# Masks from a row-xor-column table, a second bank ring for one early projection, and new TensorE costs in a list schedule

## The chip, the cores and the metric

The kernel runs on one core of a Trainium2 chip. The metric is the device time of one execution in microseconds (us); of several runs the median is given. Engines are named as in the profile: PE (TensorE), PEld (its weight loads), DVE (VectorE), ACT (ScalarE), POOL (GpSimd), SP (SyncE, which issues most DMAs).

## The reference, cut to what matters

One decoder block, 1024 tokens of width 1024, all in float32:

```python
proj = rms_norm(x, norm1_g) @ w_in            # q, k, v, hq, hf, hi, hg, two gates
o_sb = stick_breaking_attention(q, k, v)      # 8 heads of 64, strictly causal
o_hg = hgrn2_mixer(q_hg, f_hg, i_hg, g_hg)    # 4 heads of 128, a gated recurrence in chunks
mixed = sigmoid(gate_sb) * (o_sb @ w_b[:512]) + sigmoid(gate_hg) * (o_hg @ w_b[512:])
h = x + mixed @ w_out
out = h + (silu(hn @ w_gate) * (hn @ w_up)) @ w_down      # hn = rms_norm(h, norm2_g)
```

In the recurrence, `attn[t, s]` within a chunk is `sum_k q[t,k] key[s,k] exp(b[t,k] - b[s,k])` for `s <= t`, where `b` is a running sum of `log f`.

## The kernel before, in words

**Products.** A float32 product is made from three products in a rounded format (`fp32r`): each operand is split into a high part (`ah`, `oh`, `th`, ...; ACT or POOL rounds it) and a low part (`al`, `ol`, `tl`, ...; DVE subtracts). One such triple over 512 columns is the unit of the large projections. Some smaller products and all transposes run in full fp32: the transposes (through `ident`), the level products of the recurrence (`ms<-dl`), its state updates (`ms<-xi,tail`) and outputs (`ms<-tail,state`, `ms<-kb,xi`).

**Stages.** (1) x is loaded in two halves of 512 tokens, scaled by the norm's gain and split into `ah` and `al`; its squares are added up in `tail` on DVE, and a product with ones gives the sums. (2) 44 weight tiles of `w_in` give q, k, v, hq, hf, hi, hg of four pairs of heads or heads, and 16 gate tiles. Each is one call of `proj` for each half: eight steps of three matmuls into one PSUM bank. Between them run `scores`, `values` and `hgrn` for each of four steps. (3) The branch products, the output product and the FFN's first half, the latter by a Winograd scheme of seven products instead of eight. (4) The down projection, written out by hand in program order.

**The list schedule.** Stages 1 to 3 aren't issued in program order. `Plan.op` records every instruction with its engine, a planned duration, a rank and its dependencies; `Plan.issue` then simulates the engines with these durations and issues each engine's instructions in the order in which the simulation starts them. On each engine the ready instruction of highest rank goes first, then the one with the longest way to the end of its stage. The projections have rank -1 on PE, so they are filled in where nothing else is ready; an op may also have an earliest planned time (`plan.at`). The planned durations only set the order: on the chip each engine runs its queue in that order and waits by semaphores. PE's ops are made by `M` (a group of matmuls, by columns, or with a given `us`) and `T` (a group of transposes); V, A and G make those of DVE, ACT and POOL. A new duration for PE therefore changes no instruction, but may change every queue's order.

**Rings.** Buffers come from rings of fixed size, and the simulation holds an op back until there is a free one. PSUM has three: `pj` (3 banks: projections), `z` (2: scores) and `ms` (3: everything small). `tmp` has two SBUF buffers.

**The start.** The first two weight tiles (q and k of the first pair) are projected together for the first half of x, then each for the second half; all four results take a `pj` bank in turn. `take` then reads a bank with DVE into `aa` or `vx`.

**The masks.** In each of the eight recurrence steps (four heads, two halves) seven levels m = 64, ..., 1 copy a level's product into the score tile `at` (a buffer of `kb`) where a mask says that row and column lie in the same block of m (`copy_predicated` with `mk`). The seven masks of 128 x 256 bytes are made once by `level_masks` on POOL: a memset and four `affine_select` each.

**Groups by the code.** The scores have 96 steps (four pairs, two heads each, twelve tiles), each two matmuls, 16 of them 128 columns wide. The values have 22 transpose groups for each pair and 32 products over a diagonal tile in all, four matmuls each over 768 columns together. The recurrence has 16 transpose groups (`tmp`, `tail`) and 64 full-fp32 groups: 48 levels, eight state updates, eight outputs.

Of the kernel before, what the change touches and what calls it, by code (L numbers as in the profile page):

```python
# [10 lines left out]
F32 = mybir.dt.float32  # L11
F32R = mybir.dt.float32r
I8 = mybir.dt.int8
U8 = mybir.dt.uint8
AF = mybir.ActivationFunctionType
ALU = mybir.AluOpType
# [3 lines left out]
P = 128  # L20
# [203 lines left out]
def hybrid_block(ctx: ExitStack, tc, xT, wi, wb, wo, wg, wu, wd, vec, outT):  # L224
    nc = tc.nc
# [45 lines left out]
    const1 = c1.enter_context(tc.tile_pool(name="const1", bufs=1, side="right"))  # L271
    ident = const1.tile([P, P], F32, name="ident")
    ones_r = const.tile([P, P], F32R, name="ones_r")
    bones_r = const1.tile([P, P], F32R, name="bones_r")
    future = [const1.tile([P, P], I8, name=f"future{i}") for i in range(2)]
    never = const1.tile([P, P], F32, name="never")
# [43 lines left out]
    def hs(h):  # L320
        return slice(h * HALF, (h + 1) * HALF)
# [55 lines left out]

    future = [f.bitcast(U8) for f in future]


    plan = Plan()
# [29 lines left out]
    def open_pools(phase):  # L411
        def pool(name, stack, right=False):
            pools[name] = stack.enter_context(tc.tile_pool(
                name=name, bufs=1, reuse_waits="tile", **(dict(side="right") if right else {})))

        while now[0] < phase:
            now[0] += 1
            if now[0] == 2:
                c1.close()
                st1.close()  # L420
                pool("op", st2, True)
                pool("mt", st2, True)
            elif now[0] == 3:
                tst.close()
                xst.close()
                pool("wot", ctx)
                pool("mx", mst)
            elif now[0] == 4:
                st2.close()
                rst.close()  # L430
                pool("s2p", fst, True)
                pool("fp", fst, True)
            elif now[0] == 5:
                mst.close()
                pool("preB", ctx)
                pool("wA", sta)
                pool("fa", sta)

    def new(ring, shape=(P, HALF), dt=F32):
        pool, cap, tag, phase = where[ring]  # L440
        plan.ring(ring, cap)

        def make():
            open_pools(phase)
            return (pools[pool] if phase else pool).tile(list(shape), dt, tag=tag, bufs=cap, name=tag)

        return Buf(ring, make, phase)

    def fixed(tile):
        return Buf(None, lambda: tile)  # L450
# [5 lines left out]
    def V(fn, *args, n=HALF, aps=0, rank=0, part=False, holds=(), after=(), **kw):  # L456
        cycles = 2 * n if fn == nc.vector.tensor_tensor_scan else n
        us = 0.067 + cycles / 960 + 0.061 * aps
        return plan.op("V", us, [(fn, args, kw)], rank, after, part=part, holds=holds)

    def G(fn, *args, us, rank=0, after=(), holds=(), **kw):
        return plan.op("G", us, [(fn, args, kw)], rank, after, holds=holds)

    def M(cols, mms, rank=0, after=(), holds=(), us=None):

        return plan.op("P", us or cols / 2255 + 0.003 * len(mms),
                       [(nc.tensor.matmul, m[:3], dict(start=m[3], stop=m[4])) for m in mms],
                       rank, after, holds=holds)

    def T(outs, after=(), holds=()):  # L470

        return plan.op("P", 0.11 * len(outs) - 0.08, [(nc.tensor.transpose, (o, i, ident), {})
                                               for o, i in outs], 0, after, holds=holds)


# [13 lines left out]
    act, tt = nc.scalar.activation, nc.vector.tensor_tensor  # L489
    stt, ts = nc.vector.scalar_tensor_tensor, nc.vector.tensor_scalar  # L490
# [17 lines left out]

    def level_masks():

        for m in LEVELS:
            mk = const1.tile([P, 2 * P], I8, name=f"mk{m}")
            mask = fixed(mk)
            G(nc.gpsimd.memset, mask, 1.0, us=0.15, after=(last_split[0],))
            for a in range(2):
                part = mask[:, a * P:(a + 1) * P].rearrange("p (n m) -> p n m", m=m)
                G(nc.gpsimd.affine_select, out=part, in_=part, pattern=[[-m, P // m], [0, m]],
                  compare_op=ALU.is_ge, fill=0.0, base=0, channel_multiplier=1, us=0.5)
                G(nc.gpsimd.affine_select, out=part, in_=part, pattern=[[m, P // m], [0, m]],
                  compare_op=ALU.is_ge, fill=0.0, base=m - 1, channel_multiplier=-1, us=0.5)  # L520
            lvl_mask.append(mask.bitcast(U8))


# [3 lines left out]
    last_load, last_split = [None], [None]  # L527
# [14 lines left out]
    def take_w(col, early=False):  # L542
        w = new("w", (P, 1024))
        load(w, wi[col], 512)
        return [split_w(w[:, 512 * i:512 * i + 512], early) for i in range(2)]

    def take_x(h):
        ss, acc, ws, sqs = new("ms"), new("tail"), [[], []], []
        if h == 0:
            plan.ring("kb", 4)  # L550
            for u in range(2):
                w = Buf("kb", lambda u=u: first_w[u])
                hi, lo = new("oh", dt=F32R), new("ol", dt=F32R)
                plan.at[A(nc.scalar.copy, hi, w, rank=3)] = 2.4 + 0.6 * u
                V(tt, lo, w, hi.bitcast(F32), op=ALU.subtract, rank=2)
                ws[u].append((hi, lo))
        for k in range(KT):
            x = new("aa" if h == 0 else ("xf", "xq", "xi", "xg")[k // 2])
            load(x, xT[k][:, hs(h)], 256)
            if h == 0 and k in (2, 3):  # L560
                u = k - 2
                n, v = fill[u]
                w = new("kb")
                load(w, wi[COL[n] + v][:, HALF:], 256)
                ws[u].append(split_w(w, True))
            g = vt[:, V_N1 + k:V_N1 + k + 1]
            A(act, xh[k][h][:, hs(h)], x, AF.Copy, scale=g, aps=1, rank=2 - h)
            V(stt, xl[k][h][:, hs(h)], x, g, xh[k][h][:, hs(h)].bitcast(F32), op0=ALU.mult,
              op1=ALU.subtract, aps=1, rank=2 - h)
            if k == 0:  # L570
                A(act, acc, x, AF.Square, rank=1 - h)
            else:
                sq = new("ww")
                A(act, sq, x, AF.Square, rank=1 - h)
                sqs.append(sq)
        for sq in sqs:
            V(tt, acc, acc, sq, op=ALU.add, rank=1 - h)
        M(2048, [(ss, ones, acc, True, True)])
        rstd(rr[h], ss, D, rank=1 - h)
        return ws  # L580

    last_fill = [None]

    def proj(ws, h, after=None):

        pss = [new("pj") for _ in ws]
        for k in range(KT):
            cols = slice(k % 4 * P, (k % 4 + 1) * P)
            for ps, w in zip(pss, ws):
                hi, lo = w[k // 4]  # L590
                last_fill[0] = M(1536, [
                    (ps, hi[:, cols], xh[k][h][:, hs(h)], k == 0, False),
                    (ps, hi[:, cols], xl[k][h][:, hs(h)], False, False),
                    (ps, lo[:, cols], xh[k][h][:, hs(h)], False, k == KT - 1)],
                    rank=-1, after=(last_fill[0], after))
            after = None
        return pss
# [257 lines left out]
    fill = list(fill_cols)  # L855
# [11 lines left out]
    for i, (nm, u) in enumerate(fill):  # L867
        if i == 0:
            ws = take_x(0)
            take_x(1)  # L870
            level_masks()
            pss = [proj(ws, 0)] + [proj([w], 1) for w in ws]
            for (n, v), h, ps in zip(fill[:2] * 2, (0, 0, 1, 1), sum(pss, [])):
                take(n, v, h, ps)
        elif i > 1:
            plan.part = "G" if nm == "G" else "s1"
            w = take_w(COL[nm] + u, i < 4)
            for h in range(2):
                gate = None
                if nm != "G" and u:  # L880
                    d = heads[u - 1]
                    gate = d["free " + nm] if nm in "qkv" else d["free " + nm, h]
                take(nm, u, h, proj([w], h, gate)[0])
            if nm == "hg":
                plan.part = "s1"
                ends = [f(u, e) for f, e in zip((scores, values, hgrn), ends)]
# [38 lines left out]
    for i in range(KT):  # L925
        w = get_w(wb[i])
# [27 lines left out]
    for i in range(4):  # L954
# [6 lines left out]
        for e in range(2):  # L961
            k = i + 4 * e
            w = get_w(wo[seq.pop(0)])
# [308 lines left out]
```

## Time and profile before

| | us |
|---|---|
| median of three runs (lowest, highest) | 1497.53 (1497.42, 1497.81) |
| the profiled execution | 1499.36 |
| its span, first to last instruction | 1497.6 |
| PE busy in it | 1481.0 |
| DVE, ACT, POOL busy | 1197.1, 808.4, 113.2 |

Rows are read so: in the timeline, start, duration, engine, line of the code, operation, tiles written and read (buffer numbers left out), shape, count, and in brackets how long the engine was idle before it and what ended that. In groups, after the count: busy us, mean ns of one, then idle time before them. In waits: who waited for whom, us in total, times, longest. Almost every instruction of the list schedule has line 203, where `Plan.issue` calls it, so tiles tell them apart. The modelled duration of a matmul (0.39 us for 512 columns) is longer than the step from one to the next; steps are read from the starts.

### The profile page before, as it was taken

How to read it: one execution, taken by the hardware profiler on the slowest of the kernel's cores; microseconds unless marked ns; L12 is line 12 of the kernel's file. 1: busy time of each engine (PE TensorE's matmuls, PEld its weight loads, DVE VectorE, ACT ScalarE, POOL GpSimd, SP SyncE). 2: the span in 40 equal slices, each digit the busy share in tenths (PEclk: the TensorE clock that was granted, in tenths of full speed). 3: DMA queues.
4: the chain of work that ended last, by engine and by line, in shares of the span. 5: the costliest groups of instructions: out<-in, count | busy, mean ns of one | idle time of the engine just before them, and what ended most of it. 6: DMA issues, size and time to landing. Idle time of an engine off the chain costs nothing.

```text
span 1497.6 us, 20158 instructions
## 1 busy us (share of the span) xinstructions
PE 1481.0 (99%) x7021; PEld 1224.7 (82%) x7021; DVE 1197.1 (80%) x2102; ACT 808.4 (54%) x1515; POOL 113.2 (8%) x164
## 2 busy tenths in 40 slices
PE   8999999999999999999999999999999999999999
PEld 6778888888888888888888888888888888788887
DVE  9899788988899776978867798888888888575553
ACT  7976878758868877545334453333333333354442
POOL 6111101111112001100000000000000000000000
PEclk9999999999999999999999999999999999999999
DMA  5111111111111121226434345444444455797672
GB/s 183 42 52 52 62 34 47 49 40 60 51 56 47 55 68 50 70 102 242 154 112 158 103 161 174 163 162 163 163 164 167 166 169 181 263 315 228 195 222 87
DMA packets 83157, 188.50 MB, mean 126 GB/s; under 512 B 9584, under 2 KB 11632, under 8 KB 83056
## 3 DMA queue, kind: packets, MB, share of 16 engines
q1 hardware_dynamic: 72400, 167.82, 33.6%
q10 hardware_dynamic: 10656, 19.40, 3.5%
q8 instruction: 55, 0.90, 0.3%
q14 instruction: 46, 0.38, 0.1%
HBM read 131.61 MB, written 55.57 MB: 125 GB/s over the span
## 4 chain that ended last, share of the span: by engine, by line
PE 76%; DVE 8%; ACT 2%; issue 2%; DMA 0%; POOL 0%; DVEq 0%; POOLq 0%; ACTq 0%
PE pj L203 33%; PE ms L203 17%; PE f L1180 14%; PE z L203 12%; DVE dl L203 2%; DVE kb L203 1%; DVE aa L203 1%; DVE ol L203 1%; ACT aa L203 1%; DVE tl L203 1%; DVE ww L203 1%; DMA rb<-act_d 0%; ACT ww L203 0%; ACT qhh L203 0%; ACT tmp L203 0%
## 5 line engine op out<-in xcount | busy, mean ns | idle before, releaser
L203 PE MATMUL pj<-ah,oh 128*128 128x512 f32 x704 | 286.9, 407 | 1.4 <-DVE aa L203 1.0
L203 PE MATMUL pj<-al,oh 128*128 128x512 f32 x704 | 276.0, 392 | 2.2 <-DVE al L203 2.2
L203 PE MATMUL pj<-ah,ol 128*128 128x512 f32 x704 | 276.3, 392 | 0.0
L203 ACT CAST oh<-w 128x512 fp32r<-128x512 f32 x168 | 102.2, 621 | 243.4 <-PE ms L203 84.0
L203 DVE TENSOR_TENSOR ol<-w,oh 128x512 fp32r<-128x512 f32 x248 | 170.1, 690 | 15.5 <-POOL oh L203 10.3
L203 PE MATMUL ms<-f,oh 128*128 128x512 f32 x528 | 162.7, 389 | 0.2 <-DVE g L203 0.2
L203 PEld LDWEIGHTS pj<-ah,ol 128*128 128x128 f32 x704 | 132.5, 188 | 29.2
L203 PEld LDWEIGHTS pj<-al,oh 128*128 128x128 f32 x704 | 133.1, 189 | 25.7 <-DVE al L203 4.0
L203 PEld LDWEIGHTS pj<-ah,oh 128*128 128x128 f32 x704 | 133.0, 189 | 23.8 <-DVE aa L203 1.4
L1180 PE MATMUL f<-bh,ah 128*128 128x512 f32 x296 | 115.3, 389 | 1.3 <-ACT bh L256 1.3
L203 PEld LDWEIGHTS ms<-f,oh 128*128 128x128 f32 x528 | 99.0, 188 | 21.1 <-DVE g L203 0.6
L1180 PE MATMUL f<-bl,ah 128*128 128x512 f32 x296 | 115.4, 390 | 0.2 <-DVE bl L257 0.2
L1180 PE MATMUL f<-bh,al 128*128 128x512 f32 x296 | 115.1, 389 | 0.0
L203 DVE TENSOR_TENSOR_SCAN aa<-aa,ww 128x512 f32<-128x512 f32 (+3 forms) x96 | 93.0, 985 | 19.8 <-ACT aa L203 14.6
L203 PE MATMUL pj<-f,oh 128*128 128x512 f32 x352 | 108.4, 389 | 0.0
L203 PE MATMUL z<-f,oh 128*128 128x512 f32 x352 | 108.4, 389 | 0.0
L257 DVE TENSOR_TENSOR al<-ra,ah 128x512 fp32r<-128x512 f32 x73 | 50.5, 691 | 71.3 <-ACT ah L256 71.2
L203 PE MATMUL ms<-f,ol 128*128 128x512 f32 x264 | 102.7, 389 | 0.0
L256 ACT CAST ah<-ra 128x512 fp32r<-128x512 f32 x73 | 45.5, 624 | 96.8 <-PE f L1180 86.7
L203 POOL TENSOR_SCALAR oh<-w 128x512 fp32r<-128x512 f32 x80 | 62.3, 779 | 426.2 <-PE pj L203 332.7
L203 PE MATMUL pj<-mx,oh 128*128 128x512 f32 x256 | 78.8, 389 | 0.0
L203 PEld LDWEIGHTS pj<-f,oh 128*128 128x128 f32 x352 | 66.1, 188 | 13.7
(256 smaller groups left out, 3141.4 us busy)
## 6 DMA issues: line engine op xcount, KB each, us to landing
w<-wi SPq DMA_DIRECT2D x42, 512.0 KB, 3.7
rb<-act_d SPq DMA_DIRECT2D x73, 256.0 KB, 4.2
w<-wg SPq DMA_DIRECT2D x22, 512.0 KB, 3.6
w<-wu SPq DMA_DIRECT2D x22, 512.0 KB, 3.9
w<-wd SPq DMA_DIRECT2D x22, 512.0 KB, 4.6
wd_d<-ds SPq DMA_DIRECT2D x44, 256.0 KB, 2.9
ra<-wd_d SPq DMA_DIRECT2D x44, 256.0 KB, 4.2
act_d<-c SPq DMA_DIRECT2D x40, 256.0 KB, 4.7
```

What stands on the lines that cost most here:

```text
L203: fn(*[a.real() if isinstance(a, View) else a for a in args], **{k: v.real() if isinstance(v, View) else v for k, v in kw.items()})
L256: pin(nc.scalar.copy(hi, src))
L257: pin(nc.vector.tensor_tensor(lo, src, hi.bitcast(F32), op=ALU.subtract))
L1180: nc.tensor.matmul(banks[SET[o]][d], l[:, ws], r, start=start and i == 0, stop=p == NP - 1 and i == 2, skip_group_check=True)
```

## The change

```diff
+    TURN = 0.087
+
     def M(cols, mms, rank=0, after=(), holds=(), us=None):
-        return plan.op("P", us or cols / 2255 + 0.003 * len(mms),
+        short = max(0.0, 0.112 * len(mms) - cols / 2255)
+        return plan.op("P", us + TURN if us else cols / 2255 + max(short, 0.003 * len(mms)),
                        [(nc.tensor.matmul, m[:3], dict(start=m[3], stop=m[4])) for m in mms],
                        rank, after, holds=holds)

     def T(outs, after=(), holds=()):
-        return plan.op("P", 0.11 * len(outs) - 0.08, [(nc.tensor.transpose, (o, i, ident), {})
+        return plan.op("P", 0.109 * len(outs) + TURN, [(nc.tensor.transpose, (o, i, ident), {})
                                                for o, i in outs], 0, after, holds=holds)

     def level_masks():
+        apart = const1.tile([P, 2 * P], I32, name="apart")
+        column, row = (new("tmp").bitcast(I32)[:, :2 * P] for _ in range(2))
+        G(nc.gpsimd.iota, column, us=0.4, pattern=[[0, 2], [1, P]], base=0, channel_multiplier=0)
+        G(nc.gpsimd.iota, row, us=0.4, pattern=[[0, 2 * P]], base=0, channel_multiplier=1)
+        apart = fixed(apart)
+        V(tt, apart, row, column, op=ALU.bitwise_xor, n=2 * P)
         for m in LEVELS:
-            mk = const1.tile([P, 2 * P], I8, name=f"mk{m}")
-            mask = fixed(mk)
-            G(nc.gpsimd.memset, mask, 1.0, us=0.15, after=(last_split[0],))
-            for a in range(2):
-                part = mask[:, a * P:(a + 1) * P].rearrange("p (n m) -> p n m", m=m)
-                G(nc.gpsimd.affine_select, out=part, in_=part, pattern=[[-m, P // m], [0, m]],
-                  compare_op=ALU.is_ge, fill=0.0, base=0, channel_multiplier=1, us=0.5)
-                G(nc.gpsimd.affine_select, out=part, in_=part, pattern=[[m, P // m], [0, m]],
-                  compare_op=ALU.is_ge, fill=0.0, base=m - 1, channel_multiplier=-1, us=0.5)
+            mask = fixed(const1.tile([P, 2 * P], I8, name=f"mk{m}"))
+            plan.at[V(ts, mask, apart, float(m), None, op0=ALU.is_lt, n=2 * P)] = 45.0
             lvl_mask.append(mask.bitcast(U8))

-    def proj(ws, h, after=None):
-        pss = [new("pj") for _ in ws]
+    def proj(ws, h, after=None, ring="pj"):
+        pss = [new(ring) for _ in ws]
...
-            pss = [proj(ws, 0)] + [proj([w], 1) for w in ws]
+            pss = [proj(ws, 0)] + [proj([w], 1, ring=r) for w, r in zip(ws, ("pj", "z"))]
```

Two numbers lie in the same aligned block of m, a power of two, exactly when their xor is below m. So one table of row xor column (two iotas on POOL, one xor on DVE) gives all seven masks by one DVE compare each. They are held back to 45 us of planned time. POOL's 35 mask instructions go.

Of the first four projections, k's for the second half now takes a `z` bank.

In the list, n transposes are planned as 0.109 n + 0.087 us in place of 0.11 n - 0.08, and the full-fp32 groups with a given `us` get 0.087 more. A group of n matmuls given by columns is planned as at least 0.112 n. For triples of 512 columns this is the same 0.69 us as before.

More of the change, by code (lines that the diff above doesn't have):

```diff
@@ L13 @@
 I8 = mybir.dt.int8
+I32 = mybir.dt.int32
 U8 = mybir.dt.uint8
```

## The prediction

> **What bounds the kernel now.** I read the page's busy shares first, then the busy time of each engine in three stretches, then PE's waits in the first two stretches.
>
> ```profile
> PE 1481.0 (99%) x7021; PEld 1224.7 (82%) x7021; DVE 1197.1 (80%) x2102; ACT 808.4 (54%) x1515; POOL 113.2 (8%) x164
> 0.00:60.00 60.00, 54.28 (x217) 41.26 (x218) 52.01 (x95) 48.89 (x91) 26.56 (x50) 0.97 0.37 132
> 60.00:700.00 640.00, 634.37 (x3317) 529.18 (x3316) 546.73 (x1046) 468.56 (x941) 86.64 (x114) 1.00 0.20 65
> 700.00:1497.60 797.60, 792.30 (x3490) 654.30 (x3488) 598.37 (x962) 290.91 (x484) 0.00 (x0) 1.00 0.52 174
> ...
> PE pj L203 <- DVE al L203: 2.2, 2, 1.5
> ...
> PE pj L203 <- DVE aa L203: 1.0, 1, 1.0
> ...
> PE ms L203 <- DVE kb L203: 1.6, 6, 0.4
> PE ms L203 <- DVE tl L203: 1.5, 4, 0.7
> ```
>
> The columns of the stretches are PE, PEld, DVE, ACT and POOL busy, then granted clock, DMA share and GB/s. PE is the bound: it idles 5.7 us before 60 us, 5.6 us from 60 to 700 and 5.3 us after that, 16.6 of 1497.6 us. Nothing here takes work from PE, so all it can win or lose is PE's waiting. The edits act in the first two stretches: the start, where PE waits for `al` (the low half of x) and once for `aa` (a bank being read), and the body of the scheduled stage, where it waits briefly, mostly for DVE. After 700 us the planned costs are unchanged (three 512-column matmuls still plan as 0.69), so I put that part at zero; its cover is none but PE's own queue, and if it moves, it moves by a part of its 5.3 us.
>
> **The masks, at the start.**
>
> ```profile
> L203 POOL TENSOR_SCALAR_AFFINE_SELECT mk<-mk 128x128 int8<-128x128 int8 x28 | 19.9, 744 | 0.0
> L203 POOL MEMSET mk<- 128x256 int8 x7 | 2.1, 305 | 0.0
> ...
> 3.27 0.94 POOL L368 MEMSET qlz<- 64x1024 f32 x1
> ...
> 4.16 0.16 DVE L311 TENSOR_TENSOR e<-e,e 128x4 f32<-128x4 f32 x1 [0.30 <-ACT e L310]
> ...
> 4.57 0.91 DVE L313 TENSOR_TENSOR lb<-e,e 128x4 f32<-128x4 f32 x1
> 5.51 1.03 DVE L314 TENSOR_SCALAR omlb<-lb 128x4 f32<-128x4 f32 x1
> ...
> L203 DVE SCALAR_TENSOR_TENSOR al<-aa,vt,ah 128x512 fp32r<-128x512 f32 x8 | 6.8, 873 | 0.0
> L203 DVE SCALAR_TENSOR_TENSOR al<-xg,vt,ah 128x512 fp32r<-128x512 f32 x2 | 1.4, 741 | 0.0
> L203 DVE TENSOR_TENSOR ol<-kb,oh 128x512 fp32r<-128x512 f32 x4 | 3.5, 878 | 0.0
> L203 DVE TENSOR_TENSOR tail<-tail,ww 128x512 f32<-128x512 f32 x7 | 5.6, 797 | 0.3
> L203 DVE TENSOR_TENSOR tail<-tail,ww 128x512 f32<-128x512 f32 x7 | 4.8, 683 | 0.1
> ...
> 10.00:20.00 10.00, 10.00 (x42) 8.21 (x41) 9.69 (x14) 10.00 (x19) 10.00 (x15) 0.91 0.94 360
> ```
>
> 28 selects and 7 memsets, 22 us of POOL, leave. They hid under everything else except DVE, whose instructions are longer while they run: `lb` takes 0.91 and `omlb` 1.03 where the like step before takes 0.16; `al` 873 ns against 741 once POOL is idle; `tail` 797 (4.5 to 27.5 us) against 683 (later); `ol` 878 against the same 683. That is 1.6 + 8 x 0.13 + 7 x 0.11 + 4 x 0.20 = 4.2 us of DVE in rows shown, and some 1.0 more if the `al` of the second half lose as much: 5.2 us, an estimate. DVE cannot keep all of it, as ACT, which makes the inputs, is busy 10.00 of 10 us from 10 to 20; I keep two thirds, 3.4.
>
> What comes instead: two iotas on POOL, which is free of `qlz` at 4.2 us. The trace has no iota. The nearest rows for their ends are a 256-column memset, 0.31, and the 1024-column one, 0.94; I take 0.5 each, nearer the equal width. The xor then ends the wait of DVE at 4.2 + 1.0 + 0.4 = 5.6 us (4.8 to 6.5), and in the list it stands ahead of the first `ol` and `al`, so both queue behind it. The two `tmp` buffers that the iotas fill are free again at the xor, before the first gate asks for one; SP and ACT get nothing new. Then seven compares on DVE, held back in the list to 45 us, with DVE's work for q, k and v queued behind them:
>
> ```profile
> L203 DVE TENSOR_TENSOR dl<-dl,kb 128x256 f32<-128x256 f32 x56 | 23.0, 431 | 0.1
> L203 DVE TENSOR_SCALAR f<-f,vt 128x512 f32<-128x512 f32 x12 | 5.8, 483 | 0.1
> ...
> 6.86 0.89 DVE L203 SCALAR_TENSOR_TENSOR al<-aa,vt,ah 128x512 fp32r<-128x512 f32 x1
> ...
> 7.81 0.50 PE L203 MATMUL pj<-al,oh 128*128 128x512 f32 x1 [1.49 <-DVE al L203]
> ...
> 21.95 0.50 PE L203 MATMUL pj<-al,oh 128*128 128x512 f32 x1 [0.69 <-DVE al L203]
> ...
> 28.13 0.40 PE L203 MATMUL pj<-ah,ol 128*128 128x512 f32 x1
> 29.51 0.50 PE L203 MATMUL pj<-ah,oh 128*128 128x512 f32 x1 [0.98 <-DVE aa L203]
> 29.85 0.39 PE L203 MATMUL pj<-al,oh 128*128 128x512 f32 x1
> 30.08 0.40 PE L203 MATMUL pj<-ah,ol 128*128 128x512 f32 x1
> ```
>
> A compare has one tensor input; the one-input row is 0.48 for twice the columns, so it lies between half of that, 0.24, and the two-input 0.43 at its width. I take 0.3, nearer its kind: 2.1 us. The Trainium skill ("VectorE: DVE Perf Modes", Mode 2×_2P) lets a one-input instruction between SBUF tensors run two results per cycle, and "SBUF — State Buffer", Who interferes with whom, says that in this mode it blocks against GpSimd. By the first the seven would cost an estimated 1.4 us and the sum would be 0.5 lower; by the second, a POOL conversion of weights nearby could hold them up; no run here shows the compare yet.
>
> On PE: the first `al` comes at 7.75 now; behind the xor at 5.6 follow 0.7 of `ol` and 0.7 of `al`, about 7.0, so the wait of 1.49 loses 0.7. The wait at 21.95 (0.69, and 0.16 that hides in the modelled end of a matmul, busy 0.39 at a pitch of 0.23, as 29.85 to 30.08) goes: 0.85.
>
> **The fourth projection in another ring.** k's second half needs a fourth `pj` bank and gets it when DVE has read the first: 28.13 to 29.51 is 1.38 where 0.23 is normal, and the next step is 0.11 late: 1.26 us. With a bank of `z`, which the scores take only later in the list, it starts at once. Late next is then the weight for v, whose split DVE finishes earlier too.
>
> Start: 0.7 + 0.85 + 1.26 = 2.8 us earlier on PE. Against it: DVE is 3.4 earlier but then pays 2.1 for compares and is only some 1.3 ahead when the scores begin. Fill (projections whose weights are there) has to bridge the rest; I let 0.4 of it fail. If that cover were gone, the 1.5 us between PE's gain and DVE's would be lost. **Start: -2.4 us**, bounds -5 (its 5.7 idle but the unavoidable first wait) and 0 (xor at 6.5, compares all in PE's way).
>
> **The list's costs.** These issue nothing; they move the order. By the code there are 104 groups of transposes (22 a head in the values, 16 in the recurrence's inputs and keys), 64 other full-fp32 groups, 32 diagonal value products and 16 narrow scores. The question is whether the new costs are the trace's:
>
> ```profile
> 558.50 0.60 PE L203 MATMUL ms<-ident,tmp 128*128 128x128 f32 x4
> 558.86 0.36 PE L203 MATMUL ms<-th,vv 128*128 128x256 f32 x1
> 559.06 0.28 PE L203 MATMUL ms<-tl,vv 128*128 128x256 f32 x1
> 559.18 0.29 PE L203 MATMUL ms<-th,vv 128*128 128x256 f32 x1
> ...
> 650.48 0.61 PE L203 MATMUL ms<-dl 128*128 128x128 f32 x4
> 650.84 0.48 PE L203 MATMUL pj<-ah,oh 128*128 128x512 f32 x1
> 651.15 0.39 PE L203 MATMUL pj<-al,oh 128*128 128x512 f32 x1
> ```
>
> Four transposes: the next matmul starts 0.36 later (the old cost), and the one after it 0.20 later, not 0.12. Both together are 0.56, less 0.12 for the value matmul: **0.44**. The old list says 0.36, the new one 0.523. The level's fp32 group: 650.48 to 651.15 is 0.67, less 0.23: 0.44, the old cost; the new one says 0.527. So TURN books the late second step without the early first one. Transposes went from 0.08 too short to 0.08 too long, fp32 groups from right to 0.087 too long; only the short products (32 x 0.095 + 16 x 0.104 = 4.7 us) became right.
>
> What follows: where the list thinks PE slow, it lays less fill between a product and its consumer, and PE arrives before DVE. Fill comes in pieces of 3 x 0.23 = 0.69, so a consumer's spare time lies anywhere from 0 to 0.69. Taking 0.163 from it costs on average 0.163² / 1.38 = 0.02 us, 104 times 2.0; 0.087 from 64 others 0.4: 2.4 us. If two transposes and an fp32 group lie under one wait (0.41), it is 0.12 each time, over half of the 96 score steps of the code 6: with the rest 8, the upper end. The lower end takes away the 5.6 us idle of the body. DVE, whose order was drawn up for a PE too fast, now waits less for it: I credit 1.0. **List: +1.4 us.**
>
> Sum: 1497.6 - 2.4 + 1.4 = 1496.6. The execution with the profile lasted 1499.4 with 1.8 outside the span; the median of the runs is 1497.5, so 1.0 less there is **1496.5 us**.
>
> **Rivals.** *The list heals the body's waits*: the 5.6 us idle there are mostly DVE results late against a plan; if the new order removes all, 1497.5 - 2.4 - 5.6 = 1489.5. For it: 4.7 us of short products that are now right. Against: the rows above. Chance 0.26.
>
> *The clock stays up at the start.*
>
> ```profile
> 8.00:9.00 1.00, 1.00 (x4) 0.82 (x4) 1.00 (x2) 1.00 (x3) 1.00 (x3) 0.74 1.05 395
> 9.00:10.00 1.00, 1.00 (x4) 0.72 (x4) 1.00 (x3) 0.97 (x3) 1.00 (x2) 0.50 1.06 406
> ...
> 11.00:12.00 1.00, 1.00 (x4) 0.80 (x3) 1.00 (x3) 1.00 (x3) 1.00 (x3) 0.56 1.05 406
> ```
>
> From about 8.5 to 11.9 us the granted clock is 0.50, after PE's wait before 7.81. A shorter wait could leave it at full: half of 3.4 us, 1.7 less, 1494.8. If not, earlier matmuls merely run in the slow time, as my 0.7 assumes. The Trainium skill ("TensorE: Matmul & The Clock Gate", What's actually happening) has a gate that judges activity over free-running windows of 3.4 us; the length agrees with the dip here. Chance 0.10, half of it faster.
>
> *Slower: the thinner cover decides.* The double-booked turn starves PE at the score steps, +8: 1497.5 - 2.4 + 8 = 1503.1. It makes the kernel slower by 0.2% from 5.4 us on, a stall of 0.06 at each of the 96 steps. For it: DVE is busy 546.73 of 640 us and cannot hurry much. Against: a PE that waits once gives slack to what follows. Chance 0.22.
>
> **Chances.** 0.2%, 3.0 us, is what a measurement of this kernel can tell. My forecast holds 0.42, its own range 1493.5 to 1500, of which 0.04 falls under 1494.5. Faster: 0.26 + 0.05 + 0.04 = 0.35; same 0.43; slower 0.22. The range of 1489.5 to 1503 spans the cases.
>
> **What would show it.** POOL idle after its iotas until the first weights that it converts; `al` near 741 ns; no PE wait for `aa` near 29 us; the `al` wait under 1 us; seven compares near 0.3 us at some 45 us or later. For the list: more PE idle from 60 to 700 us than 5.6, at `z` and `ms` for DVE. I am wrong if that idle falls below 4 or rises over 9, or if the start keeps its 5.7 us.

## The result, and the profile after

The changed kernel takes **1513.3 us** (median of four, 1512.87 to 1513.75) beside 1497.47 before: a ratio of 1.0103 [1.0091, 1.0115], slower by 15.8 us. The profiled execution lasted 1512.87, its span 1511.2.

The page's busy shares and the three stretches of the changed kernel (columns as before: PE, PEld, DVE, ACT, POOL, clock):

```profile
PE 1487.3 (98%) x7021; PEld 1220.9 (81%) x7021; DVE 1196.5 (79%) x2110; ACT 807.3 (53%) x1515; POOL 99.1 (7%) x131
0.00:60.00 60.00, 56.37 (x234) 43.40 (x235) 51.99 (x107) 52.82 (x100) 6.50 (x19) 1.00 0.37 132
60.00:700.00 640.00, 624.52 (x3236) 511.02 (x3235) 533.35 (x1024) 455.88 (x922) 92.62 (x113) 1.00 0.18 59
700.00:1511.20 811.20, 806.45 (x3555) 666.48 (x3553) 611.14 (x981) 298.61 (x495) 0.00 (x0) 1.00 0.52 176
```

PE's idle time goes from 5.7, 5.6 and 5.3 us to **3.6, 15.5 and 4.7**. The start won, the body lost, the rest stayed. The span grew by 13.6: idle 10 - 2.1 - 0.6 = 7.3, and 6.3 more "busy" for the same 7021 matmuls. The clock in the first stretch is 1.00 instead of 0.97, worth 60 x 0.03 = 1.8, so the matmuls of the body show 8.1 more. That too is waiting: a 512-column matmul counts 0.39 where the next starts after 0.23, and when nothing follows, the other 0.16 counts as busy. So the body costs about 9.9 + 8.1 = 18 us and the start gives back some 4. The places in the trace agree: the last projection matmul (`pj<-ah,oh`) starts at 701.49 us where it started at 686.88, 14.6 later in spite of the start, and from there to the end it is 809.7 us where it was 810.8.

PE's waits from 60 to 700 us, after:

```profile
PE z L204 <- DVE ww L204: 7.9, 16, 1.7
PE ms L204 <- DVE kb L204: 3.3, 7, 0.8
PE ms L204 <- DVE tl L204: 1.7, 5, 0.5
PE ms L204 <- ACT tail L204: 1.0, 2, 0.6
```

`z` for `ww` is a score product waiting for a bank that DVE has yet to read (`ww<-z,aa`): 7.9 us in 16 waits, where the same view of the kernel before has

```profile
PE z L203 <- DVE ww L203: 0.5, 2, 0.3
```

The longest of them now, in the timeline:

```profile
366.01 0.72 POOL L204 TENSOR_SCALAR oh<-w 128x512 fp32r<-128x512 f32 x1 [2.12 <-PE pj L204]
366.23 1.03 DVE L204 TENSOR_TENSOR ol<-w,oh 128x512 fp32r<-128x512 f32 x1
367.19 0.41 DVE L204 TENSOR_TENSOR_SCAN kb<-tmp 128x128 f32<-128x128 f32 x1
...
368.88 0.68 DVE L204 TENSOR_TENSOR ol<-w,oh 128x512 fp32r<-128x512 f32 x1
369.47 0.41 DVE L204 TENSOR_TENSOR_SCAN kb<-tmp 128x128 f32<-128x128 f32 x1
369.81 0.66 DVE L204 TENSOR_TENSOR ww<-z,aa 128x512 f32<-128x512 f32 x1
...
370.52 0.38 PE L204 MATMUL z<-khl,qhh 128*128 128x256 f32 x1 [1.66 <-DVE ww L204]
```

DVE runs without a pause up to the `ww` for which PE stands. The same `ol` takes 0.96 from its start to the next while POOL converts an `oh` beside it, and 0.59 at 368.88; the list plans 0.60. (The Trainium skill, "SBUF — State Buffer", Who interferes with whom, has a DVE instruction with two SBUF inputs contend with a GpSimd instruction that reads SBUF; these rows agree.) Over all DVE instructions between 60 and 700 us that follow one another without a gap, the time from start to start, summed over the trace, is 430.0 us where the code's planned durations give 409.7: **5.0% slower than planned**. In the kernel before it is 432.4 against 414.3, 4.4%. Nearly all of that lies beside POOL. Of these instructions in the changed kernel, the 166 that overlap a POOL instruction by more than 0.05 us took 109.1 us where 91.2 are planned, 20% more; the other 673 took 320.9 where 318.5 are planned. In the kernel before it is 89.7 against 74.5, and 342.8 against 339.8.

The start, after:

```profile
4.15 0.63 POOL L204 IOTA tmp<- 128x256 int32 x2
4.29 0.22 DVE L315 TENSOR_SCALAR omlb<-lb 128x4 f32<-128x4 f32 x1
...
4.81 0.43 DVE L204 TENSOR_TENSOR apart<-tmp 128x256 int32<-128x256 int32 x1
5.15 0.68 DVE L204 TENSOR_TENSOR ol<-kb,oh 128x512 fp32r<-128x512 f32 x1
...
5.75 0.74 DVE L204 SCALAR_TENSOR_TENSOR al<-aa,vt,ah 128x512 fp32r<-128x512 f32 x1
...
6.55 0.50 PE L204 MATMUL pj<-al,oh 128*128 128x512 f32 x1 [0.33 <-DVE al L204]
...
20.38 0.50 PE L204 MATMUL pj<-al,oh 128*128 128x512 f32 x1 [0.30 <-DVE al L204]
...
25.16 0.39 PE L204 MATMUL pj<-ah,ol 128*128 128x512 f32 x1
25.38 0.39 PE L204 MATMUL z<-ah,oh 128*128 128x512 f32 x1
...
41.78 0.72 POOL L204 TENSOR_SCALAR oh<-w 128x512 fp32r<-128x512 f32 x1 [37.00 <-PE pj L204]
```

The xor starts at 4.81, `al` takes 0.74, PE waits 0.33 in place of 1.49, and the fourth projection enters its `z` bank at 25.38 with no wait. The compares:

```profile
49.80 0.69 DVE L204 TENSOR_SCALAR mk<-apart 128x256 int8<-128x256 int32 x3
50.76 1.08 DVE L204 TENSOR_TENSOR_SCAN aa<-aa,ww 128x256 f32<-128x256 f32 x2 [0.27 <-ACT aa L204]
51.75 0.60 DVE L204 TENSOR_TENSOR ww<-z,aa 128x256 f32<-128x256 f32 x2
...
52.20 0.44 PE L204 MATMUL z<-khl,qhh 128*128 128x384 f32 x1 [1.12 <-DVE ww L204]
52.26 0.68 DVE L204 TENSOR_TENSOR vv<-ms,vv 128x512 fp32r<-128x512 f32 x1
52.86 0.28 DVE L204 TENSOR_SCALAR mk<-apart 128x256 int8<-128x256 int32 x1
53.06 0.57 DVE L204 COPY_PREDICATED z<-future,never 128x128 f32<-128x128 uint8 x2
```

One takes 0.20 from its start to the next (52.86 to 53.06). The 0.27 of DVE's pause at 50.76 shows that the three at 49.80 delayed nothing.

### The profile page after: what moved, and what is told of

Its sections match the earlier page's. It is cut to its first block, busy times and chain, and to the rows that moved or that the text cites. A ratio compares the mean times of both kernels' runs of the same rounds, so it can differ in the third digit from the quotient of the medians.

```text
span 1511.2 us, 20128 instructions
## 1 busy us (share of the span) xinstructions
PE 1487.3 (98%) x7021; PEld 1220.9 (81%) x7021; DVE 1196.5 (79%) x2110; ACT 807.3 (53%) x1515; POOL 99.1 (7%) x131
## 4 chain that ended last, share of the span: by engine, by line
PE 71%; DVE 12%; ACT 6%; issue 2%; POOL 0%; ACTq 0%; DVEq 0%; POOLq 0%
PE pj L204 29%; PE ms L204 16%; PE f L1184 14%; PE z L204 12%; ACT aa L204 3%; DVE aa L204 2%; DVE dl L204 2%; DVE ol L204 1%; DVE tl L204 1%; DVE kb L204 1%; DVE ww L204 1%; ACT ww L204 1%; ACT qhh L204 1%; DVE tail L204 0%; DVE tmp L204 0%
## 5 line engine op out<-in xcount | busy, mean ns | idle before, releaser
L204 PE MATMUL pj<-ah,oh 128*128 128x512 f32 x696 | 283.1, 407 | 0.1
L204 PE MATMUL pj<-al,oh 128*128 128x512 f32 x696 | 272.1, 391 | 0.9 <-DVE al L204 0.9
L204 PE MATMUL pj<-ah,ol 128*128 128x512 f32 x696 | 272.6, 392 | 0.0
L204 PEld LDWEIGHTS pj<-ah,oh 128*128 128x128 f32 x696 | 131.1, 188 | 22.4 <-ACT ah L204 1.4
L204 POOL TENSOR_SCALAR oh<-w 128x512 fp32r<-128x512 f32 x80 | 68.1, 851 | 445.4 <-PE pj L204 349.1
L204 PEld LDWEIGHTS z<-f,oh 128*128 128x128 f32 x352 | 66.1, 188 | 13.7
```

The costliest lines, as they stand in the source:

```text
L204: fn(*[a.real() if isinstance(a, View) else a for a in args], **{k: v.real() if isinstance(v, View) else v for k, v in kw.items()})
```

## The experiments

Each kernel ran beside the kernel before on the same chip, whose medians were 1498.54, 1498.71, 1498.07, 1497.62 and 1498.44 us in the five groups below. Measured are the median, its ratio to the kernel before with a 95% interval, and PE's idle time from 60 to 700 us (640 less the PE figure of that stretch), 5.6 before and 15.5 after the change.

### First group: which part of the change

Theory A is the prediction's own finding made larger: the turn of a transpose is booked twice, PE's plan is too slow, and DVE comes late. B: any new order is a throw of dice. C: the short products do it. D: the new masks or the `z` bank do it.

**Masks and ring alone**, planned costs as before:

```diff
-        return plan.op("P", us + TURN if us else cols / 2255 + max(short, 0.003 * len(mms)),
+        return plan.op("P", us if us else cols / 2255 + 0.003 * len(mms),
...
-        return plan.op("P", 0.109 * len(outs) + TURN, [(nc.tensor.transpose, (o, i, ident), {})
+        return plan.op("P", 0.11 * len(outs) - 0.08, [(nc.tensor.transpose, (o, i, ident), {})
```

> The masks and the extra ring with the list's old costs. Theory A (the new costs book the turn twice, so PE is planned too slow and arrives early at the score steps): the start keeps its gain of some 4 us over the kernel before and the body stays near 5.6 us of PE idle, so 1492 to 1496 us. Theory B (any new order is a throw of the dice, and the order before was a lucky one): the masks move every queue too, so 1500 to 1512 us. Theory D (the compares or the z bank disturb the scores): near 1510 us, with the waits of z for ww.

1499.86, 1.0012 [1.0002, 1.0021], idle 8.0. This misses A's 1492 to 1496 and lies just under B's range. The start is as good as in the changed kernel, but what follows gives it back:

```profile
0.00:60.00 60.00, 56.75 (x232) 44.23 (x233) 51.52 (x106) 51.03 (x96) 6.64 (x18) 1.00 0.38 132
60.00:700.00 640.00, 632.01 (x3299) 524.85 (x3298) 537.52 (x1036) 464.33 (x934) 87.78 (x113) 1.00 0.19 64
```

**The list's costs alone**, masks by POOL and the fourth projection in `pj` (`level_masks` and `proj` as before; `M` and `T` as changed):

> The new list costs alone, masks and ring as before. Theory A: all of the loss and none of the start's gain, 1513 + 4 = 1515 to 1519 us, waits of z for ww as after. Theory B: anywhere from 1495 to 1515. Theory D: near 1498 us.

1518.62, 1.0132 [1.0117, 1.0147], idle 12.5. The loss is the list's; D falls. PE's waits are spread otherwise here (`ms` for `tl` 4.5 us, `z` for `ww` 3.7). A part of the loss may be this list's own: it leaves PE 4.5 us without work between 107 and 115 us of planned time, where the changed kernel's list has no gap, and in its trace the granted clock is 0.91 from 120 to 140 us.

**True transposes**: their cost as read from the trace (0.44 for four), full-fp32 groups as before, short products as changed.

```diff
-        return plan.op("P", us + TURN if us else cols / 2255 + max(short, 0.003 * len(mms)),
+        return plan.op("P", us if us else cols / 2255 + max(short, 0.003 * len(mms)),
...
-        return plan.op("P", 0.109 * len(outs) + TURN, [(nc.tensor.transpose, (o, i, ident), {})
+        return plan.op("P", 0.109 * len(outs) + 0.008, [(nc.tensor.transpose, (o, i, ident), {})
```

> As the changed kernel, but a transpose group is planned as 0.109 n + 0.008 and a full-fp32 group as before, which is what the starts in the trace of before add up to; the short products keep their new costs. Theory A: the double booking is gone, so 1494 to 1500 us. Theory B: 1500 to 1512. Theory C (it is the short products, now right, that take the cover from the scores): 1508 to 1515.

1500.83, 1.0014 [1.0004, 1.0023], idle 8.5: just above A's range and inside B's, far below C's.

**Old transposes**, the other two costs as changed (`T` alone as before, 0.11 n - 0.08):

> As the changed kernel, but the transposes keep the old cost, 0.11 n - 0.08; fp32 groups with the turn and short products as changed. Theory A: the larger part of the overbooking (104 x 0.163 of 27 us planned) is gone, so 1496 to 1504 us. Theory C: 1508 to 1515.

1500.88, 1.0013 [1.0003, 1.0022], idle 8.5. The full-fp32 groups and the short products together cost about 1 us (1500.88 against 1499.86); C falls. The transposes' cost alone makes the other 12.4. But it isn't the size of the error as such: from 0.08 too short to right costs 1 us at most (1500.83 against 1499.86, the short products included), from right to 0.08 too long some 12.

### Second group: how PE's planned pace stands to DVE's

A1: 0.08 per transpose does it, whatever DVE's plan. A2: what counts is PE's planned pace against DVE's, which is too fast by some 5%, so that the old, too short transposes stood in for it. B as above.

**DVE planned 5% slower**, all else as changed:

```diff
-        us = 0.067 + cycles / 960 + 0.061 * aps
+        us = 1.05 * (0.067 + cycles / 960 + 0.061 * aps)
```

> The changed kernel with every DVE operation planned 1.05 times as long, as DVE's back-to-back starts in the stage show it to be on average. Theory A2 (what counts is PE's planned pace against DVE's: the old, too short transposes stood in for a DVE that runs some 5% slower than planned, and the new costs took that away): DVE's planned pace now makes up for it, so 1497 to 1505 us and fewer waits of z for ww. Theory B (any order is a throw of the dice around some 1505): no pattern, 1497 to 1518, as likely above 1508 as below. Theory A1 (only the 0.08 of each transpose counts): stays at 1509 to 1515.

1497.60, 0.9994 [0.9984, 1.0003], idle 5.1. A2 holds and A1 falls: the transposes stay 0.08 too long and nearly all of the loss is gone. PE's waits at `z` for `ww` fall from 7.9 to 2.9 us.

```profile
0.00:60.00 60.00, 56.54 (x235) 43.41 (x236) 50.85 (x106) 51.46 (x96) 6.63 (x19) 1.00 0.37 132
60.00:700.00 640.00, 634.86 (x3312) 528.49 (x3311) 546.27 (x1048) 467.66 (x938) 82.62 (x113) 1.00 0.20 66
...
120.00:140.00 20.00, 20.00 (x106) 16.30 (x106) 19.22 (x45) 12.30 (x26) 3.11 (x3) 1.00 0.23 67
```

**Both**: true transposes and old full-fp32 costs as in the third run, with DVE at 1.05.

> The transposes and fp32 groups at the trace's 0.109 n + 0.008 and old cost, short products as changed, and DVE planned 1.05 times as long: both engines planned as the trace shows them. Theory A2: better than every order so far, 1490 to 1497 us. Theory A1: as with the true turn alone, 1499 to 1502. Theory B: 1497 to 1518.

1505.56, 1.0044 [1.0029, 1.0059], idle 11.1: a miss for A2. A likely reason, which no run tests by itself: here the list itself leaves PE 9.9 us without work between 100 and 150 us of planned time, with no projection ready; and the clock drops there. Its row for the stretch to hold against the last one above:

```profile
120.00:140.00 20.00, 15.64 (x71) 12.64 (x72) 16.93 (x44) 11.20 (x24) 0.46 (x1) 0.74 0.06 23
```

**Half the turn:**

```diff
-        return plan.op("P", 0.109 * len(outs) + TURN, [(nc.tensor.transpose, (o, i, ident), {})
+        return plan.op("P", 0.109 * len(outs) + 0.047, [(nc.tensor.transpose, (o, i, ident), {})
```

> The changed kernel with the transposes' turn at 0.047, half way from the true 0.008 to 0.087. Theories A1 and A2: half way between 1501 and 1513.5, so 1504 to 1510 us. Theory B: anything from 1497 to 1518.

1509.67, 1.0073 [1.0058, 1.0088], idle 12.4: at the upper end of A1's and A2's range.

**The same cost, another order** (0.001 away for four transposes; about a fifth of PE's rows change places):

```diff
-        return plan.op("P", 0.109 * len(outs) + TURN, [(nc.tensor.transpose, (o, i, ident), {})
+        return plan.op("P", 0.110 * len(outs) + 0.084, [(nc.tensor.transpose, (o, i, ident), {})
```

> The changed kernel with a transpose group at 0.110 n + 0.084 in place of 0.109 n + 0.087: a thousandth of a us apart for three and four transposes, but the order comes out different in about a fifth of PE's rows. It shows how far a new order with the same costs moves the time. Theories A1 and A2: within 4 us of the changed kernel, 1509 to 1517. Theory B: a new throw, as likely 1500 as 1515.

1514.56, 1.0106 [1.0091, 1.0121], idle 15.1. Another order with the same costs loses the same. That is one throw against B, and a smaller change of the order than the other lists make; the doses below say more.

### Third group: doses

Theory L, which the first expectation sets out, puts A2 into numbers.

```diff
-        us = 0.067 + cycles / 960 + 0.061 * aps
+        us = 1.03 * (0.067 + cycles / 960 + 0.061 * aps)
```

> The changed kernel with every DVE duration in the list times 1.03 (the earlier run had 1.05). Theory L (a ledger: what counts is how far the list overstates PE's work plus how far it understates DVE's; up to some 22 us of the two together the buffers and the fill absorb it, and above that each us costs about one): PE is overstated by 14 us (104 x 0.08 for transposes, 64 x 0.087 for full-fp32 groups), DVE understated by 1.8% of 450, 8 us; together 22, just at the edge: 1498 to 1503. Rival S (the 5% run was a lucky order; the exact number means nothing): anywhere from 1497 to 1514, most likely near the changed kernel's 1513. Rival P (proportional: three fifths of the gain of 5%): 1504.

1503.91, 1.0037 [1.0024, 1.0049], idle 9.7. The proportional rival P has it (1504); it is just above the ledger's range.

True transposes as in the first group's third run, and

```diff
-        us = 0.067 + cycles / 960 + 0.061 * aps
+        us = 1.02 * (0.067 + cycles / 960 + 0.061 * aps)
```

> Transposes at what the trace shows (0.109 n + 0.008), full-fp32 groups as before, short products as changed, DVE durations times 1.02; the new masks and the new ring. The list itself leaves PE no idle time before 700 us, unlike the run with these costs and 1.05. Theory L: PE overstated by 0, DVE understated by 2.8%, 13 us: absorbed. 1496 to 1500; the start gain of the masks and the ring shows as far as nothing takes it back. Rival S: any order is as likely to be worse, 1497 to 1506. If the hole in the list was not what made the run with 1.05 slow (1505.6), this one stays above 1502.

1498.95, 1.0006 [0.9997, 1.0015], idle 7.6. A hit for the ledger.

Twice the turn:

```diff
-        return plan.op("P", 0.109 * len(outs) + TURN, [(nc.tensor.transpose, (o, i, ident), {})
+        return plan.op("P", 0.109 * len(outs) + 0.17, [(nc.tensor.transpose, (o, i, ident), {})
```

> The changed kernel with 0.17 in place of 0.087 added to each group of transposes (n transposes plan as 0.109 n + 0.17); nothing else. Theory L: 8.6 us more overstated, so 45 us in all, 23 above what is absorbed: 1519 to 1525, with PE waiting longer from 60 to 700 us, for DVE, at z and ms. Rival (the loss saturates once the fill under each product is as thin as it gets): 1512 to 1516.

1516.64, 1.0123 [1.0107, 1.0138], idle 15.6. Slower again, but by less than the ledger said and by a little more than its rival: between the two. The ledger's 1 us for each us above the threshold is too steep here.

The old masks and ring (`level_masks` and `proj` as before) with the list costs of the second group's first run:

> The list costs of the changed kernel with DVE durations times 1.05, but the masks made by affine_select on POOL and the fourth projection in pj, as in the kernel before. Beside the run with the same list costs and the new masks and ring (1497.6) it says what the masks and the ring bring where the body does not eat the gain. If the start term holds (2.4 us, up to 5): 1500 to 1503. Rival (what the start gains is lost again later whatever the list): 1497 to 1499. The list for this kernel leaves PE 2.9 us idle between 100 and 350 us, which the other does not, so some 2 us of a difference may be that.

1502.64, 1.0030 [1.0018, 1.0041], idle 7.0. Beside 1497.60 the masks and the ring bring 5.0 us, of which some 2 may be this list's own gap. Its start, against 56.54 at a clock of 1.00:

```profile
0.00:60.00 60.00, 52.12 (x208) 39.34 (x209) 51.50 (x94) 49.08 (x91) 26.82 (x50) 0.98 0.37 132
```

4.4 of the 5.0 are PE's idle time before 60 us.

### Fourth group: the same order, another DVE

All runs so far change the order with the costs. These keep each queue exactly as it was (each instruction is planned as before) and change the real work.

**Lighter DVE in the changed kernel.** The list plans a scan; for one head of two an add is issued.

```diff
-                    V(nc.vector.tensor_tensor_scan, cw[:, ::-1], aw[:, ::-1], yw[:, ::-1],
-                      0.0 if prev is None else prev[:, 0:1], op0=ALU.add, op1=ALU.add, n=w,
-                      aps=prev is not None)
+                    plan.op("V", 0.067 + 2 * w / 960 + 0.061 * (prev is not None),
+                            [(add if e else nc.vector.tensor_tensor_scan,
+                              (cw[:, ::-1], aw[:, ::-1], yw[:, ::-1],
+                               0.0 if prev is None else prev[:, 0:1]),
+                              dict(op0=ALU.add, op1=ALU.add))])
```

> The changed kernel with every queue in exactly its order, and less real work on DVE: in the scores of the second head of each pair the 48 running sums (scans, planned at 42.6 us together) are plain adds of the same shape, which take about half as long; the list still plans them as scans. So this kernel leaves out the running sum for half of the heads. DVE has some 20 us less to do, about what it is slower than planned in the stage. Theory L (DVE's real pace against PE's in the order given is what makes PE wait): 1497 to 1503, and PE idle from 60 to 700 us falls from 15.5 to under 8. Rival S (the order as such, or PE's own queue, is bad): above 1509. Between them, 1503 to 1509, if the waits come at places that these 48 do not feed.

1506.16, 1.0054 [1.0038, 1.0069], idle 12.5. Between the two: 7.1 us come back, and the waits at `z` shrink from 7.9 us to

```profile
PE z L204 <- DVE ww L204: 4.9, 11, 1.3
```

**Heavier DVE in the kernel before.**

```diff
-                    V(tt, yw, zw, cw, op=ALU.subtract, n=w)
+                    plan.op("V", 0.067 + w / 960,
+                            [(tt, (yw, zw, cw), dict(op=ALU.subtract))] * (1 + e))
```

> The kernel before with every queue in exactly its order, and more real work on DVE: in the scores of the second head of each pair the 48 subtractions behind the running sum are issued twice (planned at 22.4 us together for one issue); the list plans them once. Theory L: DVE then is behind its plan by some 22 us more, as far from PE's planned pace as in the changed kernel: 1508 to 1518, PE idle from 60 to 700 us at 12 or more in place of 5.6. Rival S (the old order is good as such): up to 1503.

1519.29, 1.0142 [1.0128, 1.0155], idle 18.9; just above L's range. Stretch, then waits:

```profile
60.00:700.00 640.00, 621.10 (x3222) 510.45 (x3222) 554.63 (x1072) 457.37 (x925) 84.47 (x114) 1.00 0.17 56
```

```profile
PE z L203 <- DVE ww L203: 11.0, 24, 0.9
PE ms L203 <- DVE tl L203: 3.6, 4, 1.4
PE ms L203 <- DVE kb L203: 3.0, 7, 1.2
```

With the old order untouched, 48 instructions planned at 22.4 us cost 21.7, and the waits are the same kinds as in the changed kernel. So the kernel before had nothing to spare at this place, though its DVE is busy for 80% of the span. The doubled instruction is the one that frees the `z` bank, though: it adds to DVE's load and to the way from a score to the next free bank at once, and the run does not tell the two apart.

**True transposes and DVE at 1.05**, the full-fp32 groups with their TURN:

```diff
-        us = 0.067 + cycles / 960 + 0.061 * aps
+        us = 1.05 * (0.067 + cycles / 960 + 0.061 * aps)
...
-        return plan.op("P", 0.109 * len(outs) + TURN, [(nc.tensor.transpose, (o, i, ident), {})
+        return plan.op("P", 0.109 * len(outs) + 0.008, [(nc.tensor.transpose, (o, i, ident), {})
```

> The changed kernel with the transposes at what the trace shows (0.109 n + 0.008) and DVE durations times 1.05; full-fp32 groups keep their 0.087. The list leaves PE no idle time of its own before 700 us. Theory L: PE overstated by 5.6 us and DVE by nothing, the smallest distance of all runs with the new masks and ring: 1494 to 1498, under the kernel before. Rival (below some distance nothing is left to win, and what the start gains is lost elsewhere): 1497 to 1500, as the runs nearest to it.

1495.51, **0.9984 [0.9975, 0.9993]**, idle 5.5: it beats both kernels, by 2.1 and by some 18 us.

### Fifth group: the other head, the start's gain, another good list

Lighter DVE for both heads, in the changed kernel (against the first diff of the fourth group):

```diff
-                            [(add if e else nc.vector.tensor_tensor_scan,
+                            [(add,
```

> As the run with lighter work on DVE, but the running sums of both heads are plain adds (96 of 96; they are left out of the result), in exactly the changed kernel's order. Theory L: PE waits for DVE at the scores of both heads, so the second half gives as much again: 1496 to 1501, PE idle from 60 to 700 us under 8 (12.5 with one head). Rival (what is left after the first half is not DVE's throughput but the order's own, such as too little fill behind transposes): 1503 to 1506.

1497.37, 0.9992 [0.9983, 1.0001], idle 8.7 (0.7 above the bound named, with the time within). In the changed kernel's own order the time of the kernel before comes back once DVE has 40.6 us less to do (92.7 us of scans there, 52.1 of adds here, by the groups from 60 to 700 us). At `z` little is left:

```profile
PE z L204 <- DVE ww L204: 1.9, 3, 1.3
```

That is not the whole loss: the start's gain is in this time too, and the next run is 2.7 us faster with half of the lightening.

Masks and ring alone (the first group's first run) with the first diff of the fourth group:

> The run with the new masks and ring and all list costs as before (1499.9), in exactly its order, with the running sums of the second head of each pair as plain adds (left out of the result). If the start's gain is lost because PE then runs ahead of a DVE that is slower than planned: 1493 to 1497, with less idle on PE from 60 to 700 us than 8.0. Rival (it is lost elsewhere, after 700 us or in the order): 1498 to 1500.

1494.70, 0.9974 [0.9964, 0.9984], idle 6.0: 5.2 us under the same order with the scans, so the first theory holds by its range. But it also is the nearest thing to a control for the first run of the fourth group. The same 48 adds bring 5.2 us with the old costs and 7.1 with the new ones, so only some 2 of the 7.1 are owed to the new order. With equal work on DVE the two orders still lie 11.5 us apart (13.4 with the scans). The kernel before with lighter DVE, which would say what a light DVE is worth in the old order, was not run.

Another list without a gap:

```diff
-        us = 0.067 + cycles / 960 + 0.061 * aps
+        us = 1.04 * (0.067 + cycles / 960 + 0.061 * aps)
...
-        return plan.op("P", us + TURN if us else cols / 2255 + max(short, 0.003 * len(mms)),
+        return plan.op("P", us if us else cols / 2255 + max(short, 0.003 * len(mms)),
...
-        return plan.op("P", 0.109 * len(outs) + TURN, [(nc.tensor.transpose, (o, i, ident), {})
+        return plan.op("P", 0.109 * len(outs) + 0.047, [(nc.tensor.transpose, (o, i, ident), {})
```

> The changed kernel with transposes planned as 0.109 n + 0.047, full-fp32 groups as before, DVE durations times 1.04; the list has no idle time of its own on PE before 700 us. Theory L: PE overstated by 4 us, DVE understated by 0.8% (4 us), 8 together, close to the run with true transposes and 1.05 (1495.5): 1494 to 1498. Rival (that run was a lucky order): 1498 to 1503.

1498.09, 0.9999 [0.9990, 1.0008], idle 6.6: the upper edge of L's range and the lower of the rival's. A good list, but not as good as 1495.5; the ledger does not rank lists within some 2 us.

## Why the prediction was wrong, point by point

**What bounds the kernel.** "PE is the bound" was half of it. In the scheduled stage DVE, run 4 to 5% slower than the list plans, limits PE too, at the scores at least: 48 instructions more on it, planned at 22.4 us, cost 21.7. Its share of 80% does not show that; its unbroken runs before the `ww` do.

**The start** was right in its steps and too small in sum. POOL rests from 4.8 to 41.8 us, its first weight. The two iotas took 0.63 together, not 1.0; the xor starts at 4.81; the first `al` is there before 6.55, not 7.0; `al` takes 0.74 to 0.75 for all eight; the wait for `aa` is gone; the compares cost 0.20 each, so 1.4 us and not 2.1, 0.7 less where the prediction's aside has 0.5 (a 256-column xor with two inputs takes 0.34 from 4.81 to 5.15; the prediction's estimate by the Trainium skill's two results per cycle, "VectorE: DVE Perf Modes", Mode 2×_2P, was the better one). The clock stays at 1.00, the rival given 0.10. In sum 2.1 less idle and 1.8 by the clock, 3.9 us ahead at 60 us; 5.0 by the comparison of the third group, where some of the 5.0 is the list's own gap. The 0.4 for failing fill was far too low, though: with the old costs all of it was lost behind the start. That PE then only ran further ahead of a DVE that was late already fits the run with lighter DVE (1494.7); that the old list was a lucky one by some 4 us would look the same and is not ruled out.

**The list's costs** are the step that failed: +1.4 us, up to +8, against some 18. The reading of the transposes was right, 0.08 too long where they had been 0.08 too short: by the reckoning of the prediction, the median over 60 groups of four in the trace of before is 0.44, and over 30 groups of three 0.33. So was the direction: "it lays less fill between a product and its consumer, and PE arrives before DVE". The size assumed that each group's error is taken up by the fill around that group, so that only 0.02 us a group is paid. That needs a DVE that recovers between groups. The runs show an error that adds up: from the list with true transposes (1500.8) to the one with twice the turn (1516.6) PE is overstated by 22.4 us more (104 x 0.162, and 64 x 0.087), and 15.8 are paid, 0.7 of each. PE's waits are few and long, 16 at `z` for 7.9 us in the changed kernel. That PE's lead is carried from group to group until a ring is full is our reading of this; no run shows it by itself.

One reading of the list's costs was off: the short products did not become right. In the trace of before, a score of 128 columns takes 0.17 from its first start to the next product:

```profile
50.76 0.22 PE L203 MATMUL z<-khl,qhh 128*128 128x128 f32 x1
50.82 0.28 PE L203 MATMUL z<-khl,qlz 128*128 128x128 f32 x1
50.93 0.33 PE L203 MATMUL z<-khl,qhh 128*128 128x256 f32 x1
```

The old list has 0.12 for it and the new one 0.224. It went from 0.05 too short to 0.05 too long; with 1500.88 against 1499.86 that weighs little.

Nor did it help to plan the transposes as the trace has them: with DVE's durations as they were, the true cost is no better than the old one (1500.83 against 1499.86, the short products included), and what goes beyond it costs. What DVE's durations add is shown by the lists with 1.03 and 1.05, which win back what the transposes lost. The lists order roughly by what PE is overstated plus what DVE is understated (5.6 us: 1495.5; 8 to 22: 1497.6 to 1503.9; 31: 1509.7; 36: 1513.3; 45: 1516.6), with a list that runs out of projections as the exception. The kernel before does not fit in: its costs are those of the masks and ring alone, and it is as fast with a start that is some 4 us worse.

**The credit of 1.0** for a DVE that "now waits less" had the wrong sign: DVE is busy for 533.35 of the 640 us where it was for 546.73, and PE's waits for it in that stretch went from 4.9 to 13.3 us (the rows of the waits added up).

**The rivals.** The slower one, "the thinner cover decides", is what happened, at over twice its price. Its condition, DVE "cannot hurry much", fits the runs and stood in the text at 0.22. The healing rival fails: the new costs of the short products are worth nothing here (1500.88 against 1499.86).

**After 700 us** nothing changed: 4.7 of idle against 5.3.

**Open.** The lighter scans shorten both DVE's load and the way from a score to its weight, and the doubled subtraction lengthens both, so throughput and latency are not told apart. With one head's scans light, some 20 us less on DVE, more than half of the loss was still there, and most of what came back came back with the old costs too. So the runs show that the transposes' planned cost makes the loss and that DVE's planned durations can undo it; how much of it is DVE's real pace and how much an order with too little fill stays open. That DVE's 5% lies beside POOL is read from the traces; no run takes POOL's work away.

## What to carry to other kernels

In a list schedule, planned durations act as ratios between engines: before correcting those of one engine, compare the real start-to-start time of every other engine with its plan in the same stage. An engine planned too slow loses its cover; correcting the transposes and DVE together gave the fastest list here (1495.5, with the full-fp32 groups still too long), but also the one with the gap (1505.6). So look at the list's own idle time as well: where the fill ran out, the trace shows PE's idle time and a lower clock behind it. Test whether a second engine has time to spare by doubling a few of its instructions with the order held, better at a place that nobody waits for directly, and put the same change into both kernels; its share of busy time does not tell.

## What was not expected of the hardware

- A DVE subtraction with both inputs in SBUF took 0.96 us beside a POOL conversion and 0.59 alone; the planned DVE durations miss the sum by 4 to 5%, and nearly all of that is in the instructions beside POOL (20% over plan; 0.8% the others, in the changed kernel).
- An iota of 128 x 256 int32 takes about 0.31 us on POOL (two in 0.63), and a compare from int32 to int8 over 256 columns 0.20 on DVE.
- In the run with both costs corrected the clock dropped in mid-kernel, at 120 to 140 us, to 0.74 on average, where PE was idle for 4.4 of 20 us.
